# An MoE layer streamed through one core: the check for overflow tokens stands in block 0 instead of ahead of the last block

## The chip, the core and the metric

The kernel runs on one core of one Trainium2 chip. The metric is the device time in microseconds. The kernel before took a median of 740.92 us in three runs (740.85 to 742.39); the one profiled execution took 741.08 us, of which the profiler's span covers 739.1.

## What is computed

One layer over 512 tokens of width 1024: a token mixer (a gated linear recurrence beside a spatial gate, one input and one output projection), then a mixture of 32 experts with two experts for each token, and a last norm. All is float32. The part that matters here is the mixture:

```python
weights = (p_g[:, None] * top_p).reshape(-1)               # two weights per token
expert  = (g_sel[:, None] * 8 + top_i).reshape(-1)         # which expert, 0..31
...                                                        # tokens sorted by expert, any number for each
y_e     = (silu(x_e @ w1[e]) * (x_e @ w3[e])) @ w2[e]      # w1, w3: 1024x512, w2: 512x1024
out[token] += weight * y_e
```

Nothing bounds the number of tokens of one expert. All 32 experts' weights, 6.3 MB each, some 201 MB in all, are read once.

## The kernel before, in words

The front of the kernel (the mixer, the norms, the router) takes the first 235 us. From the router's logits VectorE works out, for each expert, how many tokens chose it, a token's rank within its expert, and an order of the experts by load. Fixed capacities (`CAP`) give each place in that order 32, 64 or 96 slots. 13 blocks follow (`BLOCKS`): pair blocks of two experts with 64 slots each (one has 96 and 32), and three quad blocks (2, 7 and 12) of four experts with 32 slots each. The first four experts are fixed (blocks 0 and 1); the others' numbers are read from a table into registers of SyncE (L1057).

`block` does the work of one block on TensorE: `up` multiplies the gathered tokens by w1 (h1) and w3 (h3), 32 matmuls of 512 columns for each group that the profile shows; ScalarE takes Silu of h1; VectorE multiplies it with h3 and the routing weight into `gt`; `hidden_t` transposes `gt` on TensorE and ScalarE copies it out as `gT`; `expert_out` multiplies by w2 (y, L1163) and splits the result into two parts. `transposed_onehot` makes `cT`, with which `combine_units` add a block's result to the residual x2 (L985, L986). `gather_units` build the next blocks' inputs by one-hot matmuls (L971). These units are spread between the matmul groups of later blocks as lists `along`, `early`, `before_y` and `after`; `F0` says how many of block 0's eight gather units stand ahead of its y, the rest behind it.

TensorE's and SyncE's instructions keep the order in which they are written; the others are ordered by the framework's planner. SyncE issues all weight loads (L1074), two transfers of 0.5 MB for each slot of 1 MB. A slot comes from a ring of twelve places (`RING`: five `wp`, one `l8`, two `wq`, four `ft`), and a load waits until the slot's last reader on TensorE is done. In the profile's names these are `w`, `l`, `w8q` and `w8r`. Block 0's loads and the first two slots of block 1 take the list `FIRST`; a pair block then takes exactly twelve places, so the ring stands at `ft`, `ft`, `wp` ... whenever a pair block begins.

Tokens beyond the slots are dealt with by a loop. L935 to L946 count, for each expert, the blocks of 128 tokens that are left over; the sum is `n_over`. L947 to L956 list which expert each such block belongs to (`over_id`), over a 128x512 scratch and the tile `over_e` of the front's pool `fp`. That pool is closed after the front, and the pool `ex` (with `cT` and `gT`) takes its memory. After block 11 (`OVER_AT`) every engine reads `n_over` into a register (L1283), and `tc.If(n > 0)` (L1285) guards the loop over `over_block`, which gathers up to 128 tokens, loads the whole expert through six ring slots (`weights`) and adds the result. Ahead of that check block 11's combine units are run at once. In these inputs no expert has tokens beyond its slots, so the loop is skipped.

Of the kernel before, what the change touches and what calls it, by code (L numbers as in the profile page):

```python
# [15 lines left out]
P = 128  # L16
# [15 lines left out]
OVER_AT = 11  # L32
FB, FA = 4, 3
F0 = 2
# [12 lines left out]
def trunk(ctx, tc, a, out):  # L47
# [887 lines left out]
    dve.tensor_tensor(count, count, cap, op=OP.subtract)  # L935
    nb = t2((P, 2, E))
    dve.tensor_scalar(nb[:, 0], count, 0.5, None, op0=OP.is_ge)
    for j in range(1, (S - 1) // P + 1):
        dve.tensor_scalar(nb[:, 1], count, j * P + 0.5, None, op0=OP.is_ge)
        dve.tensor_tensor(nb[:, 0], nb[:, 0], nb[:, 1], op=OP.add)  # L940
    dve.memset(nb[:, 1], 1.0)
    upto = const.tile([P, 2, E], F32, name="upto")
    dve.tensor_tensor_scan(upto[:, 1], nb[:, 1], nb[:, 0], 0.0, op0=OP.mult, op1=OP.add)
    dve.tensor_tensor(upto[:, 0], upto[:, 1], nb[:, 0], op=OP.subtract)
    n_over = const.tile([P, 1], I32, name="n_over")
    dve.tensor_copy(n_over, upto[:, 1, E - 1:E])  # L946
    over_le = t2((P, NOVER, E))  # L947
    dve.tensor_tensor(over_le, upto[:, 1:2, :].to_broadcast([P, NOVER, E]),
                      rep(slot[:, 0:NOVER], E), op=OP.is_lt)
    over_e = fp.tile([P, NOVER], F32, name="over_e")  # L950
    dve.tensor_reduce(over_e, over_le, axis=AX.X, op=OP.add)
    dve.tensor_tensor(over_le, eidx.to_broadcast([P, NOVER, E]), rep(over_e, E), op=OP.is_equal)
    dve.tensor_tensor(over_le, over_le, along(place, NOVER), op=OP.mult)
    dve.tensor_reduce(over_e, over_le, axis=AX.X, op=OP.add)
    over_id = const.tile([P, NOVER], I32, name="over_id")
    dve.tensor_copy(over_id, over_e)  # L956


# [53 lines left out]

    front.close()
# [21 lines left out]

    def weights(src, f):

        v, r = rows_of(src, f), []
        for kk in range(0, v.shape[1], 2):
            t = slot8((P, 2, D))  # L1040
            sync.dma_start(t, v[:, kk:kk + 2])
            w = t.rearrange("p k (i f) -> p (k i) f", f=f)
            r += [w[:, q, :] for q in range(w.shape[1])]
        return r
# [48 lines left out]
    def block(b, along, early, before_y, after):  # L1093
# [82 lines left out]
    def over_block(number, i):  # L1176
# [6 lines left out]
        w1, w3, w2 = [weights(a[name][0, bass.ds(e, 1)], f)  # L1183
                      for name, f in (("expert_w1", F), ("expert_w3", F), ("expert_w2", D))]
        dve.scalar_tensor_tensor(me[:, 1], upto[:, 0], 1.0, me[:, 0], op0=OP.mult, op1=OP.mult,
# [9 lines left out]
        g = g4b[:, i, :, 0:P]  # L1195
# [11 lines left out]
        spare = xT4b[i].rearrange("p (h k) s -> p h (k s)", h=2)  # L1207
# [13 lines left out]
        hs = []  # L1221
        for w in (w1, w3):
            h = bank("h")
            for k in range(KD):
                pe.matmul(h, xT[:, k, :], w[k], start=(k == 0), stop=(k == KD - 1))
            hs.append(h)
        s = t2((P, F))
        act.activation(s, hs[0], AF.Silu)
        gt = t2((P, F))
        dve.scalar_tensor_tensor(gt, s, wc, hs[1], op0=OP.mult, op1=OP.mult)  # L1230
# [3 lines left out]
        def mm(ys):  # L1234
            for q in range(FC):
                for hf, y in enumerate(ys):
                    pe.matmul(y, gT[:, q, :], w2[q][:, hf * F:(hf + 1) * F], start=(q == 0), stop=(q == FC - 1))
# [156 lines left out]
```

## Time and profile before

| | |
|---|---|
| median of 3 runs | 740.92 us |
| the profiled execution | 741.08 us, span 739.1 us |
| TensorE matmul busy | 683.0 us (92% of the span) |
| TensorE weight load busy | 362.8 us (49%) |
| VectorE busy | 298.2 us (40%) |
| ScalarE busy | 175.2 us (24%) |
| bytes moved | 246.31 MB, mean 333 GB/s |
| mean granted TensorE clock | 0.979 |

A busy share says how long an engine had an instruction, not that the kernel waits for it: matmuls are pipelined, and one that waits for the next weights counts little idle time. The slices of the page (40 equal stretches of 18.5 us) show where the transfers pause; the chain of waits, followed back from the last instruction, shows what ended each wait.

### The profile page before, as it was taken

To read this page: it belongs to the slowest core of one execution; us is meant where nothing else is said; L and a number is where in the kernel's file an instruction comes from. 1 tells how busy PE (TensorE), PEld (TensorE's weight loads), DVE (VectorE), ACT (ScalarE), POOL (GpSimd) and SP (SyncE) were. 2 spreads that over 40 slices of the span, in tenths; PEclk is the share of its full clock that TensorE was granted. 3 is DMA by queue.
4 is the path that set the end of the run, shared out by engine and by line. 5 is a ranking of instruction groups with operands and counts; after the bars stand their busy time and mean duration, and the time that the engine had idled before them with its cause. 6 is when DMAs were issued, how large, how long until landed. Compare 5 with 4: busy or idle time off the path is not lost.

```text
span 739.1 us, 10212 instructions
## 1 busy us (share of the span) xinstructions
PE 683.0 (92%) x3693; PEld 362.8 (49%) x3693; DVE 298.2 (40%) x697; ACT 175.2 (24%) x317; POOL 24.4 (3%) x55
## 2 busy tenths in 40 slices
PE   8699999999998799999999999998899999988863
PEld 7457766767886345441445445333144544443132
DVE  6359439452578813321233332221123332251025
ACT  5344496342443211100011110100001110111014
POOL 3000000000102000000000000000000000000011
PEclk9899999999999889999999999999999999999998
DMA  8999606985628869999999999999999999979993
GB/s 288 278 338 323 228 1 211 287 304 209 221 102 315 325 255 345 385 409 409 409 409 409 409 407 409 409 410 409 409 409 409 409 409 409 409 260 410 395 348 141
DMA packets 99485, 246.31 MB, mean 333 GB/s; under 512 B 14072, under 2 KB 40296, under 8 KB 99432
## 3 DMA queue, kind: packets, MB, share of 16 engines
q1 hardware_dynamic: 98152, 245.09, 88.3%
q8 instruction: 30, 0.49, 0.3%
q10 hardware_dynamic: 1056, 0.52, 0.3%
q14 instruction: 23, 0.19, 0.1%
q0 software_dynamic: 224, 0.02, 0.0%
HBM read 243.51 MB, written 2.10 MB: 332 GB/s over the span
## 4 chain that ended last, share of the span: by engine, by line
PE 43%; DMA 41%; DVE 7%; SPq 3%; ACT 3%; issue 1%; POOL 0%; ACTq 0%; DVEq 0%
DMA w8r<-in_expert_w 14%; DMA w<-in_expert_w 14%; DMA l<-in_expert_w 11%; PE h L1122 9%; PE y L1163 7%; PE c L438 4%; PE m L971 3%; PE h L438 3%; PE c L985 3%; PE m L205 2%; PE y L438 2%; DMA w<-in_ada_w 2%; SPq L261 1%; SPq L1074 1%; PE h L91 1%; PE h L92 1%
## 5 line engine op out<-in xcount | busy, mean ns | idle before, releaser
L1122 PE MATMUL h<-w,l 128*64 128x512 f32 (+1 forms) x600 | 135.0, 598 | 4.6 <-DMA w<-in_expert_w 4.5
L1122 PEld LDWEIGHTS h<-w,l 128*64 128x64 f32 (+1 forms) x600 | 37.4, 125 | 89.0 <-issue 56.5
L986 DVE TENSOR_TENSOR x<-x,c 128x512 f32<-128x512 f32 x96 | 65.5, 686 | 29.7 <-PE c L985 29.7
L985 PE MATMUL c<-l,cT 128*128 128x512 f32 x192 | 61.8, 405 | 1.9 <-DVE x L986 1.2
L1122 PE MATMUL h<-w8r,l 128*32 128x512 f32 (+1 forms) x288 | 57.6, 597 | 2.6 <-DMA w8r<-in_expert_w 2.6
L1163 PE MATMUL y<-w8r,gT 128*64 128x512 f32 (+2 forms) x272 | 53.7, 567 | 5.6 <-DMA w8r<-in_expert_w 4.9
L971 PE MATMUL m<-l,b16h 128*128 128x256 f32 (+1 forms) x192 | 51.9, 294 | 2.5 <-ACT l L818 2.5
L1010 DVE TENSOR_TENSOR t<-y,g2b 128x512 f32<-128x512 f32 x24 | 16.6, 692 | 93.1 <-PE y L1163 91.9
L87 ACT ACTIVATE l<-t 128x512 fp32r<-128x512 f32 (+1 forms) x35 | 21.3, 613 | 131.5 <-DVE t L1010 116.9
L1163 PE MATMUL y<-w8q,gT 128*64 128x512 f32 (+1 forms) x208 | 49.2, 626 | 2.1 <-DMA w8q<-in_expert_w 1.4
L1149 DVE SCALAR_TENSOR_TENSOR t<-t,ws,h 128x512 f32<-128x512 f32 x13 | 9.7, 747 | 99.3 <-PE h L1122 99.3
L971 PE MATMUL m<-l,b16l 128*128 128x256 f32 (+1 forms) x192 | 49.1, 280 | 0.0
L818 ACT ACTIVATE l<-m,s2c 128x256 f32<-128x256 f32 (+1 forms) x24 | 13.1, 547 | 145.3 <-PE m L971 145.3
L971 PEld LDWEIGHTS m<-l,b16h 128*128 128x128 f32 x192 | 36.1, 188 | 19.6 <-issue 8.1
L243 DVE TENSOR_TENSOR w8r<-w,w8r 128x512 fp32r<-128x512 f32 x48 | 30.7, 685 | 27.7 <-ACT w8r L241 27.7
L1140 DVE SCALAR_TENSOR_TENSOR ws<-m,of 128x4 f32<-128x4 f32 (+1 forms) x13 | 2.1, 163 | 91.2 <-PE m L1137 91.2
L971 PEld LDWEIGHTS m<-l,b16l 128*128 128x128 f32 x192 | 36.3, 189 | 2.5
L1122 PEld LDWEIGHTS h<-w8r,l 128*32 128x32 f32 (+1 forms) x288 | 15.6, 121 | 42.0 <-issue 26.0
L1163 PEld LDWEIGHTS y<-w8r,gT 128*64 128x64 f32 (+1 forms) x272 | 15.9, 129 | 40.2 <-issue 25.6
L241 ACT ACTIVATE w8r<-w 128x512 fp32r<-128x512 f32 x48 | 26.9, 621 | 33.9 <-PE h L93 17.6
L438 PE MATMUL c<-b16h,w8r 128*128 128x512 f32 x80 | 31.2, 415 | 3.8 <-ACT b16h L407 3.4
L1122 PE MATMUL h<-l,l 128*64 128x512 f32 (+1 forms) x136 | 32.0, 594 | 0.9 <-DMA l<-in_expert_w 0.9
(365 smaller groups left out, 953.9 us busy)
## 6 DMA issues: line engine op xcount, KB each, us to landing
w<-in_expert_w SPq DMA_DIRECT2D x160, 512.0 KB, 10.1
w8r<-in_expert_w SPq DMA_DIRECT2D x124, 512.0 KB, 10.1
w8q<-in_expert_w SPq DMA_DIRECT2D x64, 512.0 KB, 10.2
l<-in_expert_w SPq DMA_DIRECT2D x36, 512.0 KB, 10.2
w<-in_ada_w SPq DMA_DIRECT2D x32, 512.0 KB, 7.7
w<-in_w_in SPq DMA_DIRECT2D x8, 1024.0 KB, 9.6
w<-in_ada_w SPq DMA_DIRECT2D x8, 1024.0 KB, 11.1
w<-in_w_out SPq DMA_DIRECT2D x4, 1024.0 KB, 8.9
```

What stands on the lines that cost most here:

```text
L87: act.activation(hi, src, AF.Copy)
L205: pe.matmul(self.ps[32 * j:32 * j + 32], cond[:, k:k + 1].to_broadcast([P, 32]), self.w[k // 4][:, j, :], start=(k < 4), stop=(k >= 4), ti ...
L241: act.activation(hi, raw, AF.Copy)
L243: return lambda: dve.tensor_tensor(lo, raw, hi.bitcast(F32), op=OP.subtract)
L438: pe.matmul(ps[c], lhs, rhs, start=(k == 0 and n == 0), stop=(k == KD - 1 and n == 2))
L818: act.activation(o, ps, AF.Identity, scale=a2[:, k:k + 1], bias=sh2[:, k:k + 1])
L971: pe.matmul(hold[k], src[:, t, chunk(k)], g[:, t, :], start=(t == 0 and i == 0), stop=(t == NT - 1 and i == 1))
L985: pe.matmul(ps, cT[:, t, :], y[:, cs], start=(i == 0), stop=(i == 1))
L986: dve.tensor_tensor(x2[:, t, cs], x2[:, t, cs], ps, op=OP.add)
L1010: dve.tensor_tensor(yf, y, g2b[:, cs], op=OP.mult)
L1122: pe.matmul(h[c:c + n], xT[:, k, c:c + n], w[j][k], start=(k == 0), stop=(k == KD - 1), tile_position=(0, c))
L1163: pe.matmul(y[c:c + n], gT[:, q, c:c + n], w, start=(q == 0), stop=(q == FC - 1), tile_position=(0, c))
```

## The change

The list of overflow experts is no longer made in the front. The count (`over_count`, the old L935 to L946) is called within block 0, behind `gt`; then the rest of block 1's w1 and its w3 are loaded, the gather units of `before_y` and `hidden_t` follow, and then `beyond`, which holds the check. `F0` is 8, so all of block 0's gather units stand ahead of the check and of y. The loop makes the list first (`over_experts`, in memory of a token tile), uses the second half of `g4b` and `xT4b` as scratch, and takes its weights through 24 small tiles of 128x512 instead of six ring slots; behind it the one-hots and gather units of blocks 2 and 3 are made again. The check ahead of block 12 is gone, and with it the combine units of block 11 that were run at once.

```diff
-OVER_AT = 11
-F0 = 2
+F0 = 8
...
-    dve.tensor_tensor(count, count, cap, op=OP.subtract)
-    ...
-    dve.tensor_copy(n_over, upto[:, 1, E - 1:E])
-    over_le = t2((P, NOVER, E))
-    ...
-    dve.tensor_copy(over_id, over_e)
...
+    def over_count():
+        dve.tensor_tensor(count, count, cap, op=OP.subtract)
+        ...
+        dve.tensor_copy(n_over, upto[:, 1, E - 1:E])
...
         dve.scalar_tensor_tensor(gt, s, ws[:, 8:9], h3, op0=OP.mult, op1=OP.mult)
+        if b == 0:
+            over_count()
+            second[0].load()
+            second[1].load()
         for u in before_y:
             u()
         gT = hidden_t(gt)
+        if b == 0:
+            beyond(before_y)
...
-    def over_block(number, i):
+    def over_experts():
+        v = xT4b[1].rearrange("p k s -> p (k s)")
+        ...
+        dve.tensor_copy(over_id, over_e)
+    def over_block(number):
...
+        def weights(src, k):
+            t = t2((P, 512))
+            sync.dma_start(t, src[:, k // 2, (k % 2) * 512:(k % 2 + 1) * 512])
+            return t
...
+    def beyond(again):
+        by_hand.close()
+        n = nc.values_load(n_over[0:1, :], min_val=0, max_val=NOVER)
+        with tc.If(n > 0):
+            over_experts()
+            dve.memset(over_i, 0.0)
+            with tc.For_i(0, n, 1) as i:
+                over_block(bass.ds(i, 1))
+            for b in (2, 3):
+                onehots(b)
+            for u in again:
+                u()
+        by_hand.enter_context(tc.manual_schedule(engines={mybir.EngineType.PE}))
...
-        if b == OVER_AT:
-            by_hand.close()
-            for u in comb:
-                u()
-            comb = []
-            n = nc.values_load(n_over[0:1, :], min_val=0, max_val=NOVER)
-            dve.memset(over_i, 0.0)
-            with tc.If(n > 0):
-                with tc.For_i(0, n, 1) as i:
-                    over_block(bass.ds(i, 1), q % 2)
-            by_hand.enter_context(tc.manual_schedule(engines={mybir.EngineType.PE}))
```

## Rows read from the trace of the kernel before

**Rows 1.** The page's slices of 18.5 us: what the DMA engines moved.
```profile
GB/s 288 278 338 323 228 1 211 287 304 209 221 102 315 325 255 345 385 409 409 409 409 409 409 407 409 409 410 409 409 409 409 409 409 409 409 260 410 395 348 141
```

**Rows 2.** Chain of waits in order of time: start us, us, what.
```profile
303.82 9.20 DMA w8r<-in_expert_w
...
529.37 10.20 DMA w<-in_expert_w
...
627.56 7.47 PE h L1122 x32
...
715.16 8.68 DMA w<-in_expert_w
```

**Rows 3.** SyncE's waits, 310 to 540 us: us in total, times, longest us.
```profile
SPq L1074 <- DMA w<-in_expert_w: 54.9, 74, 0.9
```

**Rows 4.** Line L1283, the loads of n_over: duration ns min/median/max, first and last start.
```profile
L1283 SPq TENSOR_LOAD <-n_over x1: 277/277/277, 644.4 to 644.4; - x1
...
L1283 PEldq TENSOR_LOAD <-n_over x1: 500/500/500, 664.8 to 664.8; - x1
```

**Rows 5.** Line L1285, the check itself.
```profile
L1285 SPq EVENT_SEMAPHORE  x7: 17/17/17, 645.2 to 651.6; - x7
...
L1285 PEldq COMPARE_BRANCH  x1: 353/353/353, 665.4 to 665.4; - x1
```

**Rows 6.** SyncE's timeline, 640 to 660 us: start us, us, what, count.
```profile
640.29 4.03 SPq L1074 DMA_DIRECT2D w8r<-in_expert_w  x4
654.56 0.88 SPq L1074 DMA_DIRECT2D w<-in_expert_w  x2
```

**Rows 7.** Windows of 3 us: length, busy us by engine, PEclk, DMA share, GB/s.
```profile
648.00:651.00 3.00, 3.00 (x23) 2.69 (x22) 1.76 (x4) 1.06 (x2) 0.00 (x0) 1.00 0.62 250
651.00:654.00 3.00, 3.00 (x17) 1.17 (x17) 0.90 (x2) 0.00 (x0) 0.00 (x0) 1.00 0.10 40
654.00:657.00 3.00, 3.00 (x16) 1.01 (x14) 0.00 (x0) 0.00 (x0) 0.00 (x0) 1.00 0.48 149
657.00:660.00 3.00, 2.32 (x9) 0.74 (x6) 2.24 (x4) 1.26 (x2) 0.00 (x0) 1.00 1.03 292
```

**Rows 8.** Waits of all engines, 250 to 273 us.
```profile
PE m L999 <- ACT cT L994: 4.8, 1, 4.8
ACT cT L994 <- DVE over_id L956: 3.6, 1, 3.6
```

**Rows 9.** Chain of waits, 245 to 306 us: block 0's y and block 1.
```profile
258.93 9.70 PE y L1163 x32
268.62 2.12 PE m L971 x16
...
272.60 7.02 PE h L1122 x32
...
285.28 7.02 PE h L1122 x32
```

**Rows 10.** SyncE's timeline around block 0's y.
```profile
250.08 0.80 SPq L1074 DMA_DIRECT2D l<-in_expert_w  x2
262.65 3.39 SPq L1074 DMA_DIRECT2D w8q<-in_expert_w  x4
```

**Rows 11.** ScalarE's timeline, 250 to 258 us.
```profile
250.13 1.28 ACT L1132 ACT_TABLE_LOAD   x1 [0.49 <-PE h L1122]
251.43 0.60 ACT L1132 ACTIVATE t<-h 128x512 f32<-128x512 f32 x1
```

**Rows 12.** VectorE's groups, 244 to 260 us: busy us, mean ns, idle before.
```profile
L1149 DVE SCALAR_TENSOR_TENSOR t<-t,ws,h 128x512 f32<-128x512 f32 x1 | 0.7, 739 | 0.0
...
L943 DVE TENSOR_TENSOR_SCAN upto<-t 128x32 f32<-128x32 f32 x1 | 0.2, 225 | 0.0
```

**Rows 13.** Windows of 4 us in block 0.
```profile
258.00:262.00 4.00, 3.31 (x10) 1.00 (x10) 0.00 (x0) 0.60 (x1) 0.00 (x0) 0.50 0.00 0
262.00:266.00 4.00, 4.00 (x16) 1.22 (x14) 0.00 (x0) 0.00 (x0) 0.00 (x0) 0.72 0.60 204
```

**Rows 14.** TensorE's weight loads, 664 to 668 us: its first work behind the old check.
```profile
667.08 1.14 PEld L1296 LDWEIGHTS m<-ident,t 128*128 128x128 f32 x5 [1.99 <-issue]
```

More of the change, by code (lines that the diff above doesn't have):

```diff
@@ L932, in trunk @@
     dve.tensor_tensor(wtp[:, :, 1, :], ohs[:, :, 0, :], wtp[:, :, 0, :].bitcast(F32), op=OP.subtract)
-    dve.tensor_tensor(count, count, cap, op=OP.subtract)
[L936 to L945, printed above, removed]
-    dve.tensor_copy(n_over, upto[:, 1, E - 1:E])
-    over_le = t2((P, NOVER, E))
[L948 to L955, printed above, removed]
-    dve.tensor_copy(over_id, over_e)
     def gather_units(g, xT, ks):
@@ L1011, in expert_out @@
             split(yh[:, cs], yl[:, cs], yf)
+    upto = const.tile([P, 2, E], F32, name="upto")
+    n_over = const.tile([P, 1], I32, name="n_over")
+    over_id = const.tile([P, NOVER], I32, name="over_id")
+    def over_count():
+        dve.tensor_tensor(count, count, cap, op=OP.subtract)
+        nb = t2((P, 2, E))
+        dve.tensor_scalar(nb[:, 0], count, 0.5, None, op0=OP.is_ge)
+        for j in range(1, (S - 1) // P + 1):
+            dve.tensor_scalar(nb[:, 1], count, j * P + 0.5, None, op0=OP.is_ge)
+            dve.tensor_tensor(nb[:, 0], nb[:, 0], nb[:, 1], op=OP.add)
+        dve.memset(nb[:, 1], 1.0)
+        dve.tensor_tensor_scan(upto[:, 1], nb[:, 1], nb[:, 0], 0.0, op0=OP.mult, op1=OP.add)
+        dve.tensor_tensor(upto[:, 0], upto[:, 1], nb[:, 0], op=OP.subtract)
+        dve.tensor_copy(n_over, upto[:, 1, E - 1:E])
     front.close()
@@ L1034, in rows_of @@
         return src.rearrange("e (k p i) f -> p (e k) (i f)", p=P, i=i)
[L1036 to L1044, printed above, removed]
     experts = {}
@@ L1174, in trunk @@
     over_i = const.tile([P, 1], F32, name="over_i")
-    def over_block(number, i):
+    def over_experts():
+        v = xT4b[1].rearrange("p k s -> p (k s)")
+        le = v[:, 0:NOVER * E].rearrange("p (n e) -> p n e", e=E)
+        place, over_e = v[:, NOVER * E:(NOVER + 1) * E], v[:, (NOVER + 1) * E:(NOVER + 1) * E + NOVER]
+        dve.tensor_copy(place, expert)
+        dve.tensor_tensor(le, upto[:, 1:2, :].to_broadcast([P, NOVER, E]), rep(slot[:, 0:NOVER], E), op=OP.is_lt)
+        dve.tensor_reduce(over_e, le, axis=AX.X, op=OP.add)
+        dve.tensor_scalar(over_e, over_e, 1.0, None, op0=OP.add)
+        dve.tensor_tensor(le, along(slot[:, 0:E], NOVER), rep(over_e, E), op=OP.is_equal)
+        dve.tensor_tensor(le, le, along(place, NOVER), op=OP.mult)
+        dve.tensor_reduce(over_e, le, axis=AX.X, op=OP.add)
+        dve.tensor_copy(over_id, over_e)
+    def over_block(number):
         me = small.tile([P, 2, E], F32, name="me")
@@ L1220, in over_block @@
             scale_shift(xT[:, k, :], pt, k)
[L1221 to L1228, printed above, removed]
+        h = bank("h")
+        for k in range(KD):
+            pe.matmul(h, xT[:, k, :], weights(w1, k), start=(k == 0), stop=(k == KD - 1))
+        s = xe[:, 0:F]
+        act.activation(s, h, AF.Silu)
+        h = bank("h")
+        for k in range(KD):
+            pe.matmul(h, xT[:, k, :], weights(w3, k), start=(k == 0), stop=(k == KD - 1))
         gt = t2((P, F))
-        dve.scalar_tensor_tensor(gt, s, wc, hs[1], op0=OP.mult, op1=OP.mult)
+        dve.scalar_tensor_tensor(gt, s, wc, h, op0=OP.mult, op1=OP.mult)
         gT = hidden_t(gt)
@@ L1236, in mm @@
                 for hf, y in enumerate(ys):
-                    pe.matmul(y, gT[:, q, :], w2[q][:, hf * F:(hf + 1) * F], start=(q == 0), stop=(q == FC - 1))
+                    pe.matmul(y, gT[:, q, :], weights(w2, 2 * q + hf), start=(q == 0), stop=(q == FC - 1))
         expert_out(mm, yh, yl)
```

6 lines of the change are left out of this document (3 added, 3 removed).

## The prediction

> **What bounds the kernel now.** I read the profile from the end backwards: the page's DMA row, the chain of waits, the SyncE queue, and then the two places that the change touches.
>
> The page's GB/s row [rows 1] shows a plateau at 409 from about slice 17 to slice 34 and holes at slices 14 and 35. The chain of waits says the same: from 303.82 us to 539.57 it consists of weight transfers of 10.2 us each, and at 715.16 us it is again a weight transfer that ends it; between them, in four pair blocks, it runs over TensorE's groups [rows 2]. There both need about the same: a pair block took TensorE 30.7 us in block 1 (272.60 to 303.3) and takes the stream 12 slots of 2.55 us, 30.6. But the GB/s row stays at 409, and the start of this stretch is a transfer that lands. Between 310 and 540 us SyncE waits for older transfers of its own, 54.9 us over 74 waits for one of the four slot kinds [rows 3]. So from about 304 us on the kernel is a stream of expert weights at 409 GB/s, and TensorE follows it step by step. 8 transfers of 0.5 MB are under way at once and land 10.2 us after issue, so a slot of 1 MB (two transfers) costs 2.55 us. The end can only come earlier in two ways: the stream reaches its plateau earlier, or a hole in it closes.
>
> **The hole at the old check.** SyncE reads n_over at 644.4 us and branches past the loop [rows 4]. Its branch is followed by seven semaphore waits, from 645.2 to 651.6 us [rows 5]: seven is what the loop's body would have signalled from SyncE, six weight transfers (two for each matrix) and one register load. I read them so that the skipped path makes these signals good, and that it waits for SyncE's own latest transfers on the same semaphores first. Only then come four register loads of expert numbers, and the next weight transfer is issued at 654.56 us; the one before it belongs to the group of 640.29 to 644.32 us [rows 6]. The four windows of 3 us from 648 to 660 us ran at 250, 40, 149 and 292 GB/s [rows 7]. Against 409 that is 1.17 + 2.71 + 1.91 + 0.86 = 6.65 us of stream lost. All of it goes: without a check there, block 12 issues as block 11 did. Slots don't stop it. Without the loop's six places the ring continues with ft, ft, wp, wp, which block 11's first expert matrix freed well before. What is late next is the stream itself, 16 slots at 409 GB/s and then the last block's thinner transfers, as before; TensorE has about 14 us of work (final gain, first matrix with the combine units between) in the 20 us in which block 12's first eight slots land. So the term is **-6.65 us**, bounds -7.5 (with the restart's slow packets) and -4 (if TensorE trails in block 12).
>
> **Block 0: what goes.** In block 0 TensorE stands for 4.8 us because the transposed one-hots (cT) wait 3.6 us for over_id [rows 8]: cT takes the memory of the front pool, where over_e lay, so the list of overflow experts (L948 to L956) stands ahead of block 0's y. [...] The weight stream stands too: the last transfer of block 1's second matrix is issued at 250.08 us, the next at 262.65 [rows 10], as its slot is freed only by y's first quarter; 258 to 262 us show 0 GB/s [rows 13].
>
> In the changed kernel that list is made only inside the loop, which the data don't enter (no row of the loop's lines exists, and L1285 branches past it). The count of blocks (n_over) stays, 12 short VectorE operations of at most 0.225 us [rows 12], at most 2.7 us, now behind the gate product.
>
> **Block 0: the new order, step by step.** The up matmuls end at 250.1 us. Table load 1.28 and Silu 0.60 end at 252.0 [rows 11], the product (0.74 [rows 12]) at 252.8. On TensorE the small weight and one-hot matmuls take about 1 us and end at 251.1; then come eight gather units instead of two. Six took 272.60 - 268.62 = 3.98 us with their waits [rows 9], 0.66 each; eight end at 256.4, the four transposes 0.5 later. The check then costs TensorE a register load of 0.50 and a branch of 0.35 [rows 4, 5], with what lies between about 1.05 us; n_over is ready by about 252.8 + 2.7 = 255.5, and VectorE's own check is as long, so it isn't later than TensorE. The copy of the transposed product (0.6) lies beside the check. y begins at about **258.0 us** instead of 258.93. Bounds 256.8 (gathers at matmul speed, 0.5 us each) and 260 (a slow restart behind the jump: TensorE's idle time ahead of its first work behind the old check was 1.99 us [rows 14]).
>
> [...]
>
> SyncE's wait at the new check is covered. The loop now issues 24 transfers, so the skipped path will wait for all eight outstanding ones; the last pair, issued at 250.08 us, has landed by about 257.7, as the stream is empty in 258 to 262 [rows 13]. What is queued behind is the load of block 1's w2, which waits for y's first quarter anyway. If that cover were gone (y earlier than 256), SyncE would set the restart at about 258.
>
> First slot free: a quarter of y, 1.75 us at full clock or 3.72 us (262.65 - 258.93) as before at half. TensorE now stands for about one us instead of 4.8, so I take the middle: 258.0 + 2.7 = **260.7 us** against 262.65, bounds 258.6 and 263.7.
>
> **From there to the plateau.** The 16 slots between the check and the point where the chain becomes a pure stream (first issued at 262.65, the last one landed at 303.82 + 9.20 = 313.03) need 1.4 us to start (the window 262 to 266, behind the issue at 262.65, moved 204 x 4 = 816 KB, 2.0 us' worth, so 1.35 was lost [rows 13]) and 16 x 2.55 = 40.8 us. They took 50.4, so 8.2 us went to gaps, slow packets and the last landing. The gaps came from TensorE freeing slots late: block 1 began at 272.60 and its second matrix at 285.28 [rows 9]. With no gather units left after y, block 1 now begins at 258.0 + 7.0 to 9.7 + 0.1, so 265 to 268 us, 5 to 7.5 earlier, while the stream starts only 2 earlier. Slot 9, freed by the first quarter of the second matrix (12.7 + 1.9 = 14.6 us into the block), is free at 280 to 282, when the stream reaches it at about 283. So the gaps close; I keep 2.9 us of the 8.2 for slow packets and the landing (between 1.6 and 4.2). Slot 16 lands at 260.7 + 1.4 + 40.8 + 2.9 = 305.8 us instead of 313.0: **-7.2 us**, bounds -10.6 (258.6, loss 1.6) and -2.9 (263.7, loss 4.2). All that follows is tied to the stream and moves with it.
>
> **Sum.** -7.2 - 6.65 = -13.9 us against the profiled execution's own 741.08 (span 739.1 and 1.98 around it): 727.2. The median of the runs shown is 0.16 us lower, so 727.0. With all bounds of one side: 722.8 and 734.
>
> **Rivals.**
> *Only the hole closes.* Block 0 gives nothing, as y begins near 260 at half clock and packets stay slow: 741 - 6.65 = 734.3. For it: the clock was 0.50 in block 0's y before [rows 13], and some standing remains. Against: six gather units leave the path whatever the clock. Chance 0.11.
> *Only block 0 gains.* The end is held by TensorE in block 12, where units of combine (VectorE and TensorE in turn) sit inside the first matrix: 741.1 - 7.2 = 733.9, if it trails so far that nothing of the hole is won. Against: the 6 us of slack reckoned above. Chance 0.08.
> *The jump is dear in block 0.* All engines cross it with an empty stream, where before it lay under block 11. From this point it decides: slot 16 later than 313 + 6.65 = 319.7, so a first slot freed after 274, so a y after 272, 14 us later than reckoned. At 18 us of crossing the time is 745. Against: every engine crossed the old check within 1.1 us, with 1.99 us of idle time behind it [rows 4, 5, 14]. Chance 0.05.
> [...]
> *It doesn't do what it says*: the loop is entered in neither kernel, so its smaller tiles change nothing; if the compiled order kept the list ahead of cT, block 0 would be as before plus 1 us of check: 741.1 - 6.65 + 1 = 735.4. Chance 0.04.
>
> **How the numbers follow.** The forecast has 0.72. Its own range is 722.8 to 732; with the rivals on the same side, 8 in 10 lie in 722.5 to 734. A change under 0.2% (1.5 us) can't be told from none in this kernel. Faster by more: 0.72 + 0.11 + 0.08 + 0.02 = 0.93, of which I take 0.02 off for mixtures: 0.91. Within: 0.03. Slower: 0.06, the dear jump and a little.
>
> **What would show it.** Right: no hole near 640 to 655 us, 409 GB/s through the start of block 12; y of block 0 beginning near 258, cT no longer released by over_id; a transfer issued at 259 to 262 us and a plateau from about 265 on; block 1 beginning at 265 to 268. Wrong: TensorE or SyncE idle for several us behind the new check, the empty stretch of the stream longer than 258 to 262, or TensorE instead of weights ending the waits in block 12.

## The result and the profile after

The changed kernel takes **730.34 us** (median of 4 runs, 729.76 to 731.67) against 741.64 us of the kernel before, measured beside it (4 runs, 740.85 to 742.39): ratio 0.9855, 95% interval 0.9834 to 0.9877. The profiled execution took 730.36 us, its span is 728.6 us (before 741.08 and 739.1). Line numbers below are those of the changed kernel: up matmuls L1104, y L1151, gather units L946, SyncE's weight loads L1056, the new check L1267 (register loads) and L1268 (branch).

The page's row of what the DMA engines moved, in slices of 18.2 us, answers to [rows 1]:

```profile
GB/s 293 287 347 319 231 1 208 274 306 208 244 78 338 346 249 409 408 409 410 408 409 409 408 410 409 409 410 408 408 410 408 409 410 408 409 404 409 361 328 118
```

Two things differ. The plateau of 409 begins one slice after the dip instead of three, and the hole of 260 near the end is gone (404). A third is easy to miss: the two slices behind the plateau read 361 and 328 where before they read 395 and 348. They hold the end of the last block, whose w2 goes in packets of 1 KB, 0.046 us each (medians), where the other weights have 4 KB in 0.162 us (the thinner transfers of the prediction).

The chain of waits through block 0 (start us, us, what) answers to [rows 9]:

```profile
256.06 0.61 ACT gT L976
256.75 1.08 PE y L1151 x4
257.83 0.78 issue
258.61 6.23 PE y L1151 x28
264.84 6.87 PE h L1104 x32
...
277.37 7.02 PE h L1104 x32
...
295.93 10.35 DMA w8r<-in_expert_w
306.29 10.22 DMA w<-in_expert_w
```

y now waits for gT, not for the list of overflow experts. It begins at 256.75 us and takes 1.08 + 0.78 + 6.23 = 8.09 us instead of 9.70, at full clock (the granted clock stays 1.00 in the windows below; before it was 0.50 in 258 to 262 us [rows 13]), with a stop of 0.78 us behind its fourth matmul in which TensorE waits for nothing that is recorded. Block 1 begins at 264.84 instead of 272.60, and slot 16 lands at 306.28 instead of 313.02.

The check itself (line L1268: duration ns min/median/max, first and last start) answers to [rows 5], and SyncE's timeline behind it to [rows 10]:

```profile
L1268 SPq EVENT_SEMAPHORE  x9: 17/17/17, 256.7 to 257.3; - x9
...
L1268 SPq COMPARE_BRANCH  x1: 50/50/50, 254.1 to 254.1; - x1
L1268 PEldq COMPARE_BRANCH  x1: 352/352/352, 255.0 to 255.0; - x1
```

```profile
259.73 2.52 SPq L1056 DMA_DIRECT2D w8q<-in_expert_w  x4
```

SyncE branches at 254.1, is through the nine semaphore instructions behind it by 257.3, and then waits for the first free slot until 259.73: the check lies under the wait for the slot. Before, that transfer went out at 262.65.

Windows of the changed kernel (length; busy us and, in brackets, instructions of PE, PEld, DVE, ACT and POOL; PEclk, DMA share, GB/s): two answer to [rows 13], then the start of the last block's thin w2 transfers:

```profile
258.00:262.00 4.00, 3.39 (x16) 1.20 (x18) 0.00 (x0) 0.00 (x0) 0.00 (x0) 1.00 0.32 93
262.00:266.00 4.00, 4.00 (x22) 1.33 (x20) 1.80 (x3) 0.96 (x2) 0.00 (x0) 1.00 0.94 285
...
682.00:686.00 4.00, 3.51 (x15) 0.65 (x14) 0.00 (x0) 0.00 (x0) 0.00 (x0) 1.00 1.00 359
686.00:690.00 4.00, 3.13 (x14) 0.56 (x14) 0.00 (x0) 0.00 (x0) 0.00 (x0) 1.00 0.97 318
```

The same stretch of the kernel before:

```profile
695.00:699.00 4.00, 3.62 (x15) 0.68 (x15) 0.00 (x0) 0.00 (x0) 0.00 (x0) 1.00 1.03 391
699.00:703.00 4.00, 2.77 (x13) 0.44 (x12) 0.75 (x1) 0.00 (x0) 0.00 (x0) 1.00 1.10 349
```

Where the thin transfers begin, the share of busy DMA engines falls to 0.97 in the changed kernel and rises to 1.10 in the one before.

**A measure for the comparison.** Since the stream of weights sets the end, each trace can be read by bytes: at what time had the queue of weights moved so many MB? The table gives that time minus the one in the kernel before (us, profiled executions). Each row is counted from its own shift at 50 MB (219.5 us in the kernel before, ahead of all that the change touches), because the first 60 us differ between executions, with a lower granted clock sooner or later there (0.71 in 35 to 40 us of the changed kernel, 0.50 in run 8). Block 0 acts between 60 and 80 MB, the old hole lies at 217 to 222 MB, the last block's w2 from 234, the outputs at 244. Each row stands on one execution.

```
                       50 MB   80    120    200    215    226    240    244  | behind 226
after                   -1.2  -6.1  -6.1   -6.1   -6.1  -12.6  -11.4   -9.8  | +2.8
no check at all         +1.2  -7.8  -7.8   -7.7   -7.6  -13.9  -12.7  -11.7  | +2.2
list in loop            +0.4  -7.0  -7.0   -7.0   -7.0   -7.1   -7.1   -7.4  | -0.3
old, no check           -0.9  -0.2  -0.1   -0.2   -0.2   -6.8   -6.0   -4.6  | +2.2
28 dead matmuls         +0.2  -3.9  -3.8   -3.8   -3.9  -10.5   -9.5   -8.2  | +2.3
52 dead matmuls         +4.3  -3.6  -3.6   -3.6   -3.6  -10.3   -9.8   -8.1  | +2.2
ring turned              0.0  -6.2  -6.2   -6.1   -5.9  -11.2  -11.2   -9.3  | +1.9
pause put back          +1.1  -6.2  -6.2   -6.3   -6.3   +9.7   +9.7   +9.9  | +0.2
check at the end        -0.3  -7.5  -7.5   -7.5   -7.4  -13.9  -12.5   -0.2  | (check)
two units               +4.0  -2.8  -2.7   -2.3   -2.2   -8.4   -7.0   -5.2  | +3.2
GpSimd's code           +0.3  -5.7  -5.6   -1.5   +0.2   -6.1   -3.9   -2.8  | +3.3
```

For the changed kernel: block 0 gave 6.1 us, the hole 6.5, and behind 226 MB 2.8 are gone again. The rest of the difference of the two profiled executions (10.7 us) is about the 1.2 us of the start.

Bytes are a sum over the page's 16 DMA engines; the chain of waits runs over single transfers. So the same transfers can be compared too. SyncE issues 384 for the experts' weights, in groups that begin with the 333rd, 353rd, 365th and 377th in both kernels (start us, us, what); before, where the 333rd stands in [rows 6] at 640.29:

```profile
669.26 13.15 SPq L1074 DMA_DIRECT2D w<-in_expert_w  x10
686.02 4.06 SPq L1074 DMA_DIRECT2D w8q<-in_expert_w  x4
...
705.08 11.81 SPq L1074 DMA_DIRECT2D w<-in_expert_w  x8
```

and in the changed kernel:

```profile
633.29 9.17 SPq L1056 DMA_DIRECT2D w8r<-in_expert_w  x8
...
659.55 4.08 SPq L1056 DMA_DIRECT2D w8q<-in_expert_w  x4
...
674.91 15.49 SPq L1056 DMA_DIRECT2D w<-in_expert_w  x10
...
693.65 5.24 SPq L1056 DMA_DIRECT2D w8q<-in_expert_w  x4
```

Less the 1.2 us of the start, they go out 5.8 us earlier ahead of the hole and 8.5, 9.9 and 10.2 behind it; the very last goes out 9.9 earlier (704.09 against 715.16). So for the transfers on which the end waits, the closed hole gave 4.1 us, not 6.5, and had given it before the thin transfers began: the 2.8 us are not lost in them.

### The profile page after: what moved, and what is told of

Same layout as the page of the kernel before. It is cut to its first block, busy times and chain, and to the rows that moved or that the text cites. A ratio compares the mean times of both kernels' runs of the same rounds, so it can differ in the third digit from the quotient of the medians.

```text
span 728.6 us, 10224 instructions
## 1 busy us (share of the span) xinstructions
PE 678.5 (93%) x3693; PEld 358.9 (49%) x3693; DVE 295.6 (41%) x690; ACT 174.8 (24%) x317; POOL 24.4 (3%) x55
## 3 DMA queue, kind: packets, MB, share of 16 engines
q10 hardware_dynamic: 1056, 0.52, 0.3%
## 4 chain that ended last, share of the span: by engine, by line
DMA 60%; PE 29%; DVE 4%; SPq 3%; ACT 3%; issue 1%; POOL 0%; DVEq 0%; ACTq 0%
DMA w8r<-in_expert_w 20%; DMA w<-in_expert_w 18%; DMA l<-in_expert_w 18%; PE h L1104 4%; PE c L437 3%; PE h L437 3%; PE y L1151 3%; PE y L437 2%; PE m L204 2%; DMA w<-in_ada_w 2%; SPq L260 1%; PE h L90 1%; PE h L91 1%; PE m L946 1%; PE h L92 1%; DMA sbb<-in_sgu_b 1%
## 5 line engine op out<-in xcount | busy, mean ns | idle before, releaser
L1104 PE MATMUL h<-w,l 128*64 128x512 f32 (+1 forms) x608 | 135.5, 598 | 5.1 <-DMA w<-in_expert_w 5.0
L1104 PEld LDWEIGHTS h<-w,l 128*64 128x64 f32 (+1 forms) x608 | 37.1, 125 | 89.5 <-issue 56.6
L1104 PE MATMUL h<-w8r,l 128*32 128x512 f32 (+1 forms) x304 | 61.9, 598 | 2.8 <-DMA w8r<-in_expert_w 2.8
L946 PE MATMUL m<-l,b16h 128*128 128x256 f32 (+1 forms) x192 | 51.8, 294 | 3.2 <-ACT l L817 3.1
L1151 PE MATMUL y<-w8q,gT 128*64 128x512 f32 (+2 forms) x240 | 50.0, 570 | 3.9 <-DMA w8q<-in_expert_w 2.3
L1151 PE MATMUL y<-w8r,gT 128*64 128x512 f32 (+2 forms) x240 | 49.3, 566 | 3.2 <-DMA w8r<-in_expert_w 3.2
L946 PE MATMUL m<-l,b16l 128*128 128x256 f32 (+1 forms) x192 | 49.1, 279 | 0.0
L946 PEld LDWEIGHTS m<-l,b16h 128*128 128x128 f32 x192 | 36.1, 188 | 19.6 <-ACT l L817 8.3
L1104 PEld LDWEIGHTS h<-w8r,l 128*32 128x32 f32 (+1 forms) x304 | 16.3, 120 | 44.8 <-issue 26.0
L946 PEld LDWEIGHTS m<-l,b16l 128*128 128x128 f32 x192 | 36.3, 189 | 2.5
L960 PEld LDWEIGHTS c<-l,cT 128*128 128x128 f32 x192 | 29.2, 189 | 6.7 <-issue 3.4
L1114 ACT ACTIVATE t<-h 128x512 f32<-128x512 f32 x13 | 7.8, 598 | 99.4 <-PE h L1104 99.4
## 6 DMA issues: line engine op xcount, KB each, us to landing
w8r<-in_expert_w SPq DMA_DIRECT2D x124, 512.0 KB, 10.2
w8q<-in_expert_w SPq DMA_DIRECT2D x64, 512.0 KB, 10.2
```

The costliest lines, as they stand in the source:

```text
L946: pe.matmul(hold[k], src[:, t, chunk(k)], g[:, t, :], start=(t == 0 and i == 0), stop=(t == NT - 1 and i == 1))
L960: pe.matmul(ps, cT[:, t, :], y[:, cs], start=(i == 0), stop=(i == 1))
L1104: pe.matmul(h[c:c + n], xT[:, k, c:c + n], w[j][k], start=(k == 0), stop=(k == KD - 1), tile_position=(0, c))
L1151: pe.matmul(y[c:c + n], gT[:, q, c:c + n], w, start=(q == 0), stop=(q == FC - 1), tile_position=(0, c))
```

## The experiments

**1. No check at all.** The changed kernel without count, branch and loop.

```diff
-            over_count()
...
-        if b == 0:
-            beyond(before_y)
```

> The changed kernel without count, check and loop (tokens beyond the slots are left out; these inputs have none). Theory: the check in block 0 lies beside the copy of the transposed product, and only the 0.78 us stop of TensorE after y's first four matmuls belongs to it; so block 0's restart comes 0.5 to 1.5 us earlier, and the time falls from 730.3 to 729 or 729.8, unless the last block's code lands on other fetch points, which can give or take 1 to 3 us. Rival (the check is dear in block 0): the time falls by more than 3 us up to the plateau, byte for byte.

730.70 us (730.23 to 731.56), ratio to before 0.9868 [0.9848, 0.9889]: the same as the changed kernel. The two profiled executions took 730.36 us each, though this one started 2.4 us later (first column of the table). y runs through without a stop, as the chain shows:

```profile
259.18 7.09 PE y L1148 x32
```

By bytes block 0 gains 7.8 instead of 6.1 us, so the check in block 0 costs about 1.7 us there, 0.8 to 1.0 of it the stop inside y (8.09 against 7.09). The medians don't show it: it stands on one execution of each. And although nothing of a check is left, 2.2 us are again gone at the end: that loss has nothing to do with code of the check.

**2. The list alone.** The kernel before with the list of overflow experts made inside the loop; check and pause stay at block 11.

```diff
-    over_le = t2((P, NOVER, E))
...
+                over_experts()
                 over_block(bass.ds(i, 1), q % 2)
```

> The kernel before with one part of the change: the list of overflow experts is made inside the loop, the check stays ahead of block 12. Theory: cT no longer waits for over_id, y of block 0 begins 3 to 4 us earlier at full clock (1.00), the stream is 4 to 5 us earlier from 80 MB on, and the hole at 650 us stays: 736 to 738 us. Rival (the list is beside the path, all of the gain is the hole): 741 to 742 us.

733.93 us (732.89 to 734.86), ratio 0.9906 [0.9884, 0.9929]. By bytes -7.0 us from 80 MB on and -7.4 at the outputs: behind 226 MB nothing is lost. y begins at 254.84 us and runs at full clock:

```profile
254.84 7.09 PE y L1154 x32
```

So taking the list out from ahead of block 0 is enough for block 0's gain, and gives more than the whole change does there (6.1) and than the 4 to 5 us that I had expected; run 1, with eight units ahead of y, has 7.8.

**3. The hole alone.** The kernel before without check and loop, its list still ahead of block 0.

```diff
-        if b == OVER_AT:
-            by_hand.close()
...
-                    over_block(bass.ds(i, 1), q % 2)
```

> The kernel before without the check and the loop ahead of block 12 (tokens beyond the slots are left out; these inputs have none); the list is still made in the front. Theory: the hole closes, 6.5 us of stream, and block 0 stays as it was: 734 to 736.5 us, depending on whether the last block loses 1 to 3 us as in the changed kernel. Rival (TensorE holds the end once the hole is closed): 738 us or more, with TensorE and not weights ending the waits of block 12.

735.39 us (733.49 to 738.19), ratio 0.9932 [0.9911, 0.9954]. The hole gives 6.6 us at its place and 2.2 of them are gone at the end: net 4.4. So the late loss belongs to the closed hole, with block 0 as it was. Runs 2 and 3 have one part of the change each, run 1 both without the check: -7.4 and -4.6 at the outputs, together -12.0, against -11.7.

**4. and 11. Code that is never run.** 28 and 52 matmuls at the end of the loop's body, which the branch skips.

```diff
+        pt = bank("m", (P, P))
+        for i in range(28):
+            pe.matmul(pt, ident, ident, start=True, stop=True)
```

> The changed kernel with 28 more matmuls at the end of the loop's body, which no run here enters: only the addresses of TensorE's code behind the loop move, by about 112 instructions. Theory: the last block's loss of 1.2 us (685 to 694 us) and the tail's 1.4 us (one DMA engine late behind 709 us) come from fetches of TensorE's code that fall at the start and the end of the last weights; with the fetches moved some 100 instructions earlier both go: 727.5 to 729 us. Rival (the loss comes from the other order of slots in the last block): 730 to 730.8 us, no change.

> The changed kernel with 52 matmuls that are never executed at the end of the loop body (28 of them made 734.3 us): the branch in block 0 skips a longer stretch of TensorE's code, and its target lies at another place. Theory A (behind the taken branch TensorE runs what has already been fetched and stops for the rest, so the stop depends on where the target lies in what was fetched): another stop than the 0.8 us of the changed kernel, between none and 3.5 us, with a code fetch on record right before TensorE goes on: 729.5 to 734.5 us, y and the restart late by as much. Theory C (the longer skipped stretch itself costs, in proportion): more than with 28, 735.5 to 738.

734.29 us (733.34 to 734.98; ratio 0.9917 [0.9897, 0.9936]) and 735.96 us (732.29 to 738.86; 0.9917 [0.9889, 0.9944]): 4 us and more above the changed kernel, part of it by the start of the executions (first column of the table), so that by its time alone run 11 falls into theory C's range. TensorE's timeline of the kernel with 28 (start, us, operation, in brackets the idle time before it and what ended it; PEq is TensorE's sequencer):

```profile
256.79 0.60 PE L974 MATMUL m<-ident,t 128*128 128x128 f32 x4
260.41 5.35 PE L1151 MATMUL y<-w8q,gT 128*64 128x512 f32 x16 [3.02 <-PEq L1271]
```

and of the one with 52:

```profile
264.49 5.35 PE L1151 MATMUL y<-w8q,gT 128*64 128x512 f32 x16 [2.90 <-PEq L1271]
```

With the dead code TensorE stands 3.02 and 2.90 us between the transposes and y, where the check lies; in the changed kernel it went on after 0.73, when gT was there, and stopped 0.78 us four matmuls later. The branch itself shows where the time goes: 3.71 and 3.59 us on TensorE, against 0.35 in the changed kernel (with 28, then with 52; ns):

```profile
L1271 PEldq COMPARE_BRANCH  x1: 3706/3706/3706, 256.4 to 256.4; - x1
L1271 PEldq COMPARE_BRANCH  x1: 3592/3592/3592, 260.6 to 260.6; - x1
```

Fetches of 16 KB of code lie in those stretches (257.4 us with 28, 261.6 with 52), and the granted clock falls (0.75 in 262 to 266 us with 28, 0.69 in 266 to 270 with 52), so that y takes 8.79 and 8.78 us. By bytes block 0 gives 3.9 and 3.6 instead of 6.1. The length of the skipped stretch isn't the price, as 52 cost no more than 28. That the place of the target in what has been fetched sets the stop (run 11's theory A) fits two lengths of the branch, but isn't shown: a fetch of 16 KB begins 1.0 us behind the start of both long branches, and one begins at 256.1 us in the changed kernel too, 1.1 us behind the start of its short one. The late losses are there as before (2.3 and 2.2), though the fetches have moved; the theory of run 4, that single code fetches happen to fall into the last block's start (727.5 to 729 us), fell with that.

**5. Another order of the buffers.** In the last block the changed kernel gets its buffers in another order than the kernel before, whose loop took places of the ring. Here the ring is turned back.

```diff
+        if last:
+            slots[0:2] = []
+            slots.extend(RING[4:])
```

> The changed kernel with the ring of weight buffers turned by six places ahead of the last block, so that this block gets its tiles in the order that it has in the kernel before (there the loop under the check took places of the ring). In the kernels whose pause at the old check is closed, the bytes of the last block and the outputs come 2 to 2.8 us later than the rest of the stream says; in the kernels with the pause they don't. Theory A (the DMA engines drift apart: in the changed kernel the 16 completions of one transfer lie 6.1 us apart around 650 us, in the kernel before 1.8 us after its pause; what the slowest engine is behind is paid at the end): the order of the buffers is nothing, 729.5 to 731.2 us, the spread at 650 us again about 6, the loss over the last 8 MB again 2 to 3 us. Theory B (the order of the buffers in the last block): the loss goes, 727.0 to 728.5 us.

730.60 us (730.27 to 732.12), ratio 0.9854 [0.983, 0.9878]: no gain, so the order is not the cause. By bytes it is instructive. Turning the ring makes SyncE wait once for a later buffer, a pause of 1.2 us between 217 and 222 MB (-5.9 to -11.2 instead of -6.1 to -12.6), and the loss of 1.2 us between 226 and 240 MB is gone. At the outputs the pause cost 0.5 us (-9.3 against -9.8), less than its length.

**6. A pause without a check.** In block 11 SyncE reads a word that VectorE writes when that block's combine is done; its combine units are run at once, as in the kernel before.

```diff
+            dve.tensor_scalar(held, x2[:, NT - 1, D - 1:D], 0.0, None, op0=OP.mult)
+            nc.values_load(held[0:1, :], engines=[mybir.EngineType.SP], min_val=0, max_val=NOVER)
```

> The changed kernel with only a pause put back where the old check stood: after block 11 SyncE reads one word that VectorE writes once that block's combine is done; no branch, no loop, no code moved. Theory A (drift of the DMA engines): the pause of 6 to 7 us in the stream levels the engines (spread after it under 2.2 us instead of 5 to 6), the loss in the last block and the tail goes, and so the pause costs only 3.5 to 4.5 us net: 733.5 to 735. Theory B (the order of the buffers in the last block, which stays the changed kernel's here): the pause costs its full 6.5 us: 736.3 to 737.5, and the loss in the last block stays.

752.36 us (751.82 to 752.96), ratio 1.015 [1.0129, 1.0171]. Neither number fits, since the pause came out far longer than the old one. SyncE's waits, and the page's GB/s row:

```profile
SPq L1308 <- DVE held L1307: 23.4, 1, 23.4
```

```profile
GB/s 284 279 337 309 224 1 225 280 313 210 186 149 299 284 372 409 409 409 409 409 408 409 408 409 409 410 408 410 409 410 408 410 409 408 149 172 412 395 348 131
```

What the theories say of the end can still be read: behind the pause the last two slices are 395 and 348, exactly those of the kernel before, and by bytes 0.2 instead of 2.8 us are lost behind 226 MB, with the changed kernel's order of buffers. Against the changed kernel the pause took 22.3 us of the stream (226 MB) and 19.7 at the outputs. So this pause ahead of the last block took the loss away.

**Why a pause does that.** The trace holds 16 completions for each transfer; I take them for one of each of the page's 16 DMA engines. The time from the first to the last of them is then how far the engines have drifted apart (means over 10 transfers, of the four semaphores of which all completions are on record): before, 1.5 us at 267 to 295 us, growing to 5.2 at 607 to 629, then the hole, and 1.8 at 663 to 686. In the changed kernel 1.7 at 266 to 288, 6.2 at 601 to 623, and still 6.1 at 653 to 675, 5.1 in the last block. With the list alone (hole kept) 5.0, then 1.8; with the turned ring 5.8, then 4.1; behind the long pause 0.8. In the kernel before, from 316 to 650 us, the spread rose from 2.2 to 5.9 us and fell nowhere by more than 0.15 from one transfer to the next; behind the hole, at 660 us, it was 1.0. I read this as an engine that stays behind while the stream runs without a gap, and catches up in a gap while the others stand. SyncE issues a transfer when an older one has landed whole ([rows 3]; in the changed kernel from 310 to 689 us its next issue comes 0.12 us behind a last completion, the median of 147 transfers), so the issues, and the chain of waits, follow the slowest engine. A hole of 6.65 us that costs them 4.1 fits that: by these two numbers the slowest engine made good some 2.5 us on the mean of all in it, an estimate, and the spread from first to last fell by 3.4 (5.2 to 1.8). The chain of the changed kernel (start us, us, what):

```profile
605.64 10.92 DMA w8r<-in_expert_w
616.57 10.22 DMA w<-in_expert_w
...
647.24 10.91 DMA w<-in_expert_w
658.16 10.23 DMA l<-in_expert_w
```

Most links between 300 and 680 us are 10.2 us, and seven are 10.5 to 10.9. Each of the seven has a packet of the queue of 8 KB code fetches in it or 0.2 us ahead of it (429.4, 472.8, 492.3, 518.3, 563.8, 608.5 and 649.6 us; 0.32 us each, median); the three earlier ones (342.5, 387.9, 407.9) have no long link. The spread steps up at the same packets, from 3.5 to 4.2 us at 472.8 and from 5.0 to 5.8 at 563.8. The 16 KB packets of TensorE's code (30 on their queue, 31 with run 11's 52 matmuls, and still 30 with run 12's code for GpSimd), fifteen of about 1.08 us here, don't do that: the spread doesn't move at the five from 356.7 to 438.2, and three of the fifteen lie in a long link, as many as chance would give. So the theory of runs 9 and 12, that each fetch of 16 KB sets an engine back by 0.7 us, put it down to the wrong queue. Why a packet of 0.32 us costs up to 0.7 isn't shown.

**7. The check at the end.** Behind the last block's up projections, when all weights have been issued.

```diff
-        if b == 0:
-            beyond(before_y)
...
     by_hand.close()
+    beyond()
```

> The changed kernel with the check neither in block 0 nor ahead of the last block but behind the last block's up projections, after the last weights have been issued; its scratch lies in the other half of the gather buffers, so that nothing is made again behind the loop. Theory A (in block 0 the check costs 1.5 to 2 us by TensorE's stop for code behind the branch and the late restart, and drift of the engines is paid at the end in any case): the bytes between 78 and 217 MB come 1 to 2 us earlier than in the changed kernel, and if the branch at the end hides under the last w2 transfers, 728 to 730; if TensorE stops for code there as well, 730 to 732. Theory B (the check in block 0 is covered, its stop of 0.78 us is all it costs): 729.5 to 730.5, no shift of the middle of the stream over 0.8 us.

740.07 us (737.40 to 742.70), ratio 0.9983 [0.9961, 1.0005]. Block 0 gains 7.5 us, as without a check, and the tail loses 12: outputs at -0.2 against -12.5 at 240 MB. The waits of 700 to 722 us (engine, line, waited for: us in total, times, longest):

```profile
DVE t L1320 <- SPq L1265: 21.0, 1, 21.0
ACT L86 <- DVE t L1320: 20.1, 1, 20.1
```

VectorE's work on the last block waits for SyncE's side of the check, and SyncE has it behind it only at 712.4 us, 9.5 us after its last issue. Without that, the last block's y and combine run while its weights still come in. Neither of my numbers allowed for it.

**8. Two units instead of eight ahead of y.** `F0 = 2` as before, the check in block 0.

```diff
-F0 = 8
+F0 = 2
```

> The changed kernel with two, not eight, of the gather units of the next pair ahead of the y matmuls of block 0 (as the kernel before has it), the check still in block 0. Theory A (what the eight units do is to cover the count and the check; without them y begins once gT and the branch are done): y begins 2 to 4 us earlier, near 253 to 255 us, but TensorE meets the branch before SyncE and VectorE have got to it and stands for code behind it, and the six units that moved behind y delay block 1: between 728.5 and 732. Theory C (the eight units are what holds y back, so the early start is all gain, since the stream waits for the first free slot): 726.5 to 728.5, first free slot 2 to 4 us earlier.

735.57 us (730.51 to 740.21, a wide spread; the profiled execution is the slowest), ratio 0.9904 [0.9875, 0.9932]: above both ranges, 4.0 us of the profiled one by its start. TensorE's timeline:

```profile
259.82 6.53 PE L1151 MATMUL y<-w8q,gT 128*64 128x512 f32 x16 [2.52 <-PEq L1268]
```

its load of the count, and the window behind it (columns as above):

```profile
L1267 PEldq TENSOR_LOAD <-n_over x1: 487/487/487, 258.6 to 258.6; - x1
...
262.00:266.00 4.00, 4.00 (x12) 1.22 (x10) 0.00 (x0) 0.00 (x0) 0.00 (x0) 0.54 0.34 116
```

TensorE is done with its transposes at 257.3 us and stands 2.52 us: VectorE has the count ready at 258.5, the load follows at 258.6 and takes 0.49 us, and y begins some 0.7 us behind its end; a branch of 3.6 us, as in runs 4 and 11, isn't in it. The granted clock then falls to 0.54 in 262 to 266 us, and six gather units follow y, which begins at 259.82, not at 253 to 255. Together with runs 1 and 2 this gives block 0 as a square, by bytes at 80 MB: two units without a check -7.0, with it -2.8; eight units without a check -7.8, with it -6.1. The check costs 4.2 us uncovered and 1.7 behind eight units. Neither F0 nor the place of the check can be judged alone.

**9. and 10. Small extra transfers.** 22 copies of 8 KB issued by ScalarE in blocks 1 to 11, as one row and as sixteen rows.

```diff
+        if 0 < b < NB - 1:
+            for i in (2 * b, 2 * b + 1):
+                act.dma_start(extra[i:i + 1], a["x"][0, 2 * i:2 * i + 2] ...)
```

> The changed kernel plus 22 small transfers issued by ScalarE, two in each of blocks 1 to 11, each one row of 8 KB copied to memory that nobody reads: 0.18 MB in all beside 243 MB, so by the mean rate of 409 GB/s worth 0.4 us (0.9 with the second way). Theory A (a transfer in one piece sets one DMA engine back, as TensorE's 16 KB code fetches do by 0.7 us each, and the stream's end waits for the engine that is furthest behind): each row sets an engine back by about 0.35 us; if they all fall on the same engine it gets 7 to 8 us further behind, the spread of one transfer's 16 completions grows well beyond the 6 us of the changed kernel and the time goes up by 3 to 8 us (733 to 738); if they take turns over the engines, 0.4 to 1.5 us. Theory C (only bytes count, the spread is harmless): 730.3 to 731.3.

> The same 22 transfers of the same 8 KB, but each as sixteen rows of 512 bytes, which can be shared out over the 16 DMA engines. Theory A (drift): no engine is set back against the others, the spread is that of the changed kernel and the time 730.3 to 731.5 us, clearly below the kernel with one row each if there all rows fall on one engine. Theory C: the same as with one row, 730.3 to 731.3.

739.41 us (736.35 to 741.71; ratio 0.9965 [0.9946, 0.9984]) and 739.40 us (736.90 to 741.59; 0.9969 [0.995, 0.9989]). Inconclusive. In both the page has the same 1760 packets on ScalarE's queue (1056 in the changed kernel), so 704 / 22 = 32 packets a copy: the one row was cut up as well, and the two runs don't differ in what they were to test. And the extra 9 us lie in the front: in the first 10 us ScalarE is busy 0.00 us (6.66 in the changed kernel), so both were 9 and 8 us late at 50 MB. I don't know why. From there on they come out 8.7 and 9.2 us ahead of the kernel before, much like the changed kernel's 9.8.

**12. More code fetches, no more work.** In each of blocks 1 to 11 GpSimd, which stands still in the stream, runs 256 tiny instructions. VectorE waits 5.4 us in all for the copies among them, off the chain of waits.

```diff
+            pool.tensor_copy(tick, x2[:, NT - 1, D - 1:D])
+            for _ in range(255):
+                pool.memset(tick[0:1], 0.0)
```

> The changed kernel plus work for GpSimd alone, which stands still in the stream: in each of blocks 1 to 11 one word copied and 255 words set to zero, 2816 instructions that nobody waits for, so some 11 more code fetches of 16 KB or 22 of 8 KB during the stream (0.18 MB, by bytes 0.4 us). Theory A (each code fetch sets one DMA engine back, by 0.7 us for 16 KB and some 0.35 us for 8 KB, and the end of the stream waits for the engine furthest behind): the spread of one transfer's 16 completions before the last block goes from the changed kernel's 6 us to 7 to 10 us, the last block and the tail lose 0.5 to 4 us more, 731 to 734.5 us, while the middle of the stream keeps its 409 GB/s. Theory C (the spread costs nothing, or does not come from code fetches): the spread stays at 6 us, and 730.3 to 731.3 us.

739.10 us (737.21 to 741.01), ratio 0.997 [0.9952, 0.9989]: slower than the changed kernel by far more than expected. The page's GB/s row and its row of the queue of 8 KB code fetches (packets, MB, share), of which the changed kernel has 25:

```profile
GB/s 289 282 340 319 229 1 203 280 300 211 242 86 318 342 273 409 409 408 409 409 409 408 409 409 396 395 410 402 399 391 406 401 394 402 379 401 410 354 326 119
...
q14 instruction: 47, 0.39, 0.1%
```

22 more packets of 8 KB, 0.18 MB, and the plateau breaks at slice 24. Until about 423 us the stream runs at 409 GB/s, as the windows say (columns as above), then at 399:

```profile
300.00:423.00 123.00, 118.45 (x714) 51.13 (x708) 36.17 (x63) 14.33 (x24) 74.75 (x837) 1.00 1.03 409
423.00:669.00 246.00, 235.77 (x1160) 101.52 (x1156) 70.12 (x120) 27.11 (x46) 149.62 (x1671) 1.00 1.02 399
```

The changed kernel in the same windows:

```profile
300.00:423.00 123.00, 119.38 (x718) 52.02 (x710) 36.16 (x63) 14.32 (x24) 0.00 (x0) 1.00 1.03 409
423.00:669.00 246.00, 235.83 (x1176) 102.18 (x1174) 72.90 (x124) 27.12 (x46) 0.00 (x0) 1.00 1.03 408
```

TensorE, VectorE and ScalarE are as busy as without GpSimd's work. The drift grows about twice as fast: 6.6 us at 427 to 449 us, where the changed kernel has 3.3, and it grows in steps of 0.6 to 0.7 at the 8 KB packets (331.0, 349.8, 368.5 and 424.8 us, for instance). Then it stays at 5.8 to 6.8 while the stream goes at 399 GB/s, 5.8 us lost between 120 and 215 MB; that the whole stream then goes at the pace of the engine furthest behind is my reading, not shown. The chain has 20 long links instead of seven, each with at least one of the 31 packets of 8 KB in it (start us, us, what):

```profile
571.38 10.72 DMA l<-in_expert_w
582.11 10.19 DMA w8r<-in_expert_w
592.32 10.71 DMA w<-in_expert_w
603.04 11.26 DMA l<-in_expert_w
```

So in this run 22 more fetches of 8 KB made more drift, and the drift went with lost time. The direction was right; the size (731 to 734.5) was not, as I had not expected the stream itself to slow down, as it did here at a spread of 5.8 to 6.8 us.

## Why the prediction was right, and where its terms were not

The direction held, and both places gave time for the reasons named; the forecast was 727.0 us, the measured time 730.34. The sum was 13.9 us and the change gave 9.8 in the profiled executions, counted from 50 MB.

*The hole, -6.65.* At its place 6.5 by bytes, and the cause is the check: run 3 takes only that away and gains 6.6 there. As a gain at the end the term was too large: 4.1 us by the issues of the same transfers, 4.4 at the outputs in run 3.

*"All of it goes ... What is late next is the stream itself ... and then the last block's thinner transfers, as before."* This step failed. I took the hole as pure loss. It was also the one gap in 380 us in which the DMA engines got level again (the spread fell from 5.2 to 1.8 us), and that is worth 2 to 3 us at the end (runs 1, 3, 5, 6). The pause of 6.65 us cost the issues 4.1, not its length. The thin transfers themselves ran as before: by the issues the gain is 9.9 us ahead of them and 9.9 at the last one, where SyncE waited 1.3 us for a place that y held, a wait that the kernel before doesn't have.

*Block 0, -7.2.* Measured 6.1 by bytes, 5.8 by the issues (slot 16 landed 6.7 earlier, 1.2 of it the start). y began 7.9 us behind the last up matmul, as reckoned. The clock was 1.00, better than "the middle". Against that stand the stop of 0.78 us behind the branch, and the slow restart (93 and 285 GB/s in the two windows from 258 to 266 us). Block 1 began 16.0 us behind the up matmuls' end, where I had 15 to 18. The bounds of -10.6 and -2.9 held.

*SyncE's wait is covered.* Right: done at 257.3, needed at 259.7.

*The rivals.* "The jump is dear" showed at a smaller size: not 14 us and more, but 0.8 here and a branch of 3.6 to 3.7 us with other code (runs 4, 11), too little to turn the sign. "Only the hole closes" and "only block 0 gains" are what runs 3 and 2 make, 735.4 and 733.9 us; I had 734.3 and 733.9. The first is off by the drift again.

So of the 13.9 us, by bytes, the hole missed 0.15, block 0 1.1, and what the hole had levelled cost 2.8; that the executions differ by 10.7 in place of 9.8 is the start, 1.2 us earlier in this one, not the change. The bound of -4 on the hole just covers the 4.1 us, but by luck: the reason given for it, TensorE trailing in block 12, isn't what took most of the difference.

## What to carry to other kernels

Where a stream of transfers sets the time, look at the spread of a transfer's completions over the DMA engines before pricing a hole: here closing 6.65 us gained 4.1 at the issues, as the pause had levelled some 2.5. Put a check that all engines must cross where each of them waits anyway, and price it by the engine that gets there first: here the same check cost 4.2 us where TensorE had to wait for the count, and 1.7 where eight units stood ahead of it. Instructions off the path were fetched too, beside the data: in run 12, with 22 more packets of 8 KB, the stream fell to 399 GB/s, where the changed kernel kept 408.

## What the runs showed of the hardware that I had not expected

- One fetch of 16 KB of TensorE's code took 1.08 us, one of 8 KB 0.32 us (medians). In the changed kernel's stream of 4 KB packets without gaps it is at the 8 KB ones that an engine falls behind, by 0.3 to 0.7 us in the links of the chain. TensorE's own fetches don't show in the chain: from 306 to 689 us, with fifteen of them, it holds landings and nothing of TensorE. For the stream of weights the 8 KB fetches do show: 22 packets, 0.18 MB or 0.4 us by bytes, cost 7 us in run 12's profiled execution, counted from 50 MB.
- In run 12 the spread stopped growing at 5.8 to 6.8 us, with 8 transfers of 10.2 us under way, and from there the stream itself slowed from 409 to 399 GB/s. In the changed kernel it came to 6.2 us and the stream kept 408.
- Code that is never entered made block 0 slower by 2.2 and 2.5 us (by bytes), through a branch of 3.71 and 3.59 us on TensorE and the lower granted clock after it (0.75 and 0.69).
- A check behind the last issued weights held VectorE for 21.0 us, until SyncE's last semaphore of the skipped path at 712.4 us.
